# A decoder layer whose input is normalised after the products: roots applied at PSUM, embedding projection moved to the end, one set of gate logits

## The chip, the cores and the metric

The kernel runs on one core of a Trainium2 chip. The metric is device microseconds of that core for one execution, median of several runs. TensorE (PE) multiplies matrices into PSUM; VectorE (DVE), ScalarE (ACT) and GpSimd (POOL) do the element work; SyncE (SP) issues the DMAs.

## The reference, cut to what matters

One decoder layer on 1088 tokens: 1024 of a prompt and 8 x 8 of running samples, width 1024.

```python
proj = rmsnorm(h, norm_mix) @ w_in
qkv, z, b_logit, a_logit, sq, sk, sv, gates = jnp.split(proj, cuts, axis=-1)
o_a, conv_new, s_new = gdn_branch(qkv, z, b_logit, a_logit, ...)   # short conv, silu, gated delta rule, 8 heads
o_b, k_new, v_new = swa_branch(sq, sk, sv, ...)                    # window of 128, 16 query heads on 4 key heads
gates = jax.nn.sigmoid(gates)
h = h + (gates[..., :D] * o_a + gates[..., D:] * o_b) @ w_out
hid = jax.nn.relu(rmsnorm(h, norm_ffn) @ w_up)
h = h + (hid * hid) @ w_down
h = h + jax.nn.sigmoid(rmsnorm(h, norm_ple) @ w_ple_gate) * (p_l @ w_ple_proj)
```

`rmsnorm(x, w)` is `x * rsqrt(mean(x*x) + EPS) * w`: one inverse root per token. It commutes with the product over features: `rmsnorm(x, w) @ W` is `(x * w) @ W` with each token's row times its root.

## The kernel before

Activations lie with features on the 128 partitions and the 1088 tokens along the free dimension, in three chunks of 384, 384 and 320 tokens (`CH`). Every product is done in a split format: an operand is a high part `xh` and a low part `xl`, a weight likewise `wh` and `wl`, and three products (lines 166 to 168) add up high by high, high by low and low by high. A weight tile of 128 output features is used by 8 x 3 products for each chunk. `order` lists all weight tiles; `next_w` keeps three raw loads and one split ahead, and the split costs one ACT copy (L134) and one subtraction (L135, POOL from the third tile on).

Instructions are put in a fixed order per engine when the kernel is built; an engine then works through its own order and waits at semaphores. So what stands behind a waiting instruction on an engine waits too. `side` holds small steps that are dealt out between the products of a tile.

The stages, in order:

1. Head. The embeddings `pT` are split, and `ple(f)` projects them with `wpp` for eight feature tiles; ACT takes each chunk from PSUM (`ppo`, L328) and a DMA stores it in DRAM (`ppd`). Beside that `x_norm(i)` does the input norm of a chunk: ACT squares (L306), DVE sums (L309), `rsqrt_pe` (PE column sums L247, POOL power L251, a ladder of diagonals `dg` L256 and products L257 that spread the roots over the partitions), then x is scaled by root and weight (L316) and split into `xs` (L317, L318).
2. Gate logits: 48 narrow products (L388), transposes (L427, L430), and `gates_tm` twice, once for the prompt and once for the samples, each a chain of small DVE operations; then decay sums by PE (L435 to L454) and a pass through DRAM (`gcd`).
3. Keys. Eight `conv_steps` tiles: ACT takes the chunk from PSUM (`raw`, L500, L502), conv and silu follow. `key_rows` and `key_products` prepare the matrices `kk`, `E` and `LT` of the delta rule. Two feature tiles (`evac_to`, L350) follow.
4. Solve and queries (some 242 to 392 us). Two more tiles by `evac_to` (`qf`, L350) and eight query tiles (`swa_q`, L799 to L805) run on PE, while DVE solves triangular systems in `LT` (`substitute`, L666, L667).
5. Attention (some 392 to 612 us). Eight gate tiles (`gate_tile`, ACT takes the tanh straight from PSUM, L1075), with the attention's steps as side work: scores (L930, L931), DVE scaling and maximum (L934 to L938), exponent on ACT (L940), transposes (L953), values (L975). `swa_keys` and `swa_queries` prepare split keys (`klo`, L888) and queries.
6. Eight delta-rule heads (`gdn_head`): four projection tiles each, the scan as side work.
7. Output projection, norm, MLP in eight blocks, norm, and the gate of the embeddings: for each feature tile `pr` is read back from `ppd`, `ut` is PSUM times root (L1450), tanh, `(ut + 1) * pr` (L1452), added to `h` and stored.

PSUM has eight banks: three `pg` (`ps`) for projections, two `psc`, two `pst`, one `psn`.

## Time and profile before

| | |
|---|---|
| median of 3 runs | 2144.08 us (2135.99 to 2146.12) |
| profiled execution | 2146.7 us |
| its span, first to last instruction | 2144.9 us |
| mean granted PE clock | 0.983 |
| busy: PE, weight loads, DVE, ACT, POOL | 2079.6, 1995.2, 1071.9, 795.5, 718.0 us |
| DMA | 196.5 MB, 92 GB/s mean |

In rows of groups stand line, engine, operation, output and inputs with their shapes, count, then busy time and mean nanoseconds of one, and the idle time before them with what ended it. In rows of waits: who waited, for whom, total us, times, longest. In rows of the timeline: start, duration, engine, line. Products are pipelined, so a product's duration is longer than its share of the engine: the distance between starts is its price.

### The profile page before, as it was taken

How to read it: one execution, taken by the hardware profiler on the slowest of the kernel's cores; microseconds unless marked ns; L12 is line 12 of the kernel's file. 1: busy time of each engine (PE TensorE's matmuls, PEld its weight loads, DVE VectorE, ACT ScalarE, POOL GpSimd, SP SyncE). 2: the span in 40 equal slices, each digit the busy share in tenths (PEclk: the TensorE clock that was granted, in tenths of full speed). 3: DMA queues.
4: the chain of work that ended last, by engine and by line, in shares of the span. 5: the costliest groups of instructions: out<-in, count | busy, mean ns of one | idle time of the engine just before them, and what ended most of it. 6: DMA issues, size and time to landing. Idle time of an engine off the chain costs nothing.

```text
span 2144.9 us, 33830 instructions
## 1 busy us (share of the span) xinstructions
PE 2079.6 (97%) x13597; PEld 1995.2 (93%) x13597; DVE 1071.9 (50%) x1717; ACT 795.5 (37%) x1951; POOL 718.0 (33%) x676
## 2 busy tenths in 40 slices
PE   6999999789999999999999999999999999999999
PEld 6899899668889999999998999999999999999999
DVE  6444499787654555445555444233332323333654
ACT  6476433477643443344334322212131212212411
POOL 3332456243235545454455222212121212121211
PEclk9999999899999999999999999999999999999999
DMA  6365443343243223322242221111111111111132
GB/s 238 122 216 183 116 147 109 104 125 114 85 142 97 76 93 123 108 92 77 93 151 75 77 69 50 40 50 40 50 40 50 40 50 41 49 43 47 40 127 80
DMA packets 89065, 196.50 MB, mean 92 GB/s; under 512 B 33613, under 2 KB 44749, under 8 KB 88781
## 3 DMA queue, kind: packets, MB, share of 16 engines
q1 hardware_dynamic: 88908, 194.35, 27.7%
q8 instruction: 107, 1.75, 0.3%
q14 instruction: 50, 0.40, 0.1%
HBM read 145.48 MB, written 50.78 MB: 91 GB/s over the span
## 4 chain that ended last, share of the span: by engine, by line
PE 80%; DVE 11%; ACT 4%; issue 3%; POOL 2%; DMA 1%; SPq 0%; ACTq 0%; DVEq 0%; POOLq 0%
PE ps L166 23%; PE ps L168 22%; PE ps L167 22%; DVE fs L666 3%; DVE LT L667 3%; PE psn L975 1%; PE pst L953 1%; DVE nm L938 1%; PE psc L1285 1%; ACT pst L572 1%; PE psc L1216 1%; PE psn L1297 1%; PE psc L1290 1%; PE psc L1280 1%; ACT pr L940 1%
## 5 line engine op out<-in xcount | busy, mean ns | idle before, releaser
L135 POOL TENSOR_TENSOR wl<-wr,wh 128x1024 fp32r<-128x1024 f32 x140 | 343.4, 2453 | 909.1 <-ACT wh L134 893.8
L166 PE MATMUL ps<-xh,wh 128*128 128x384 f32 (+1 forms) x1800 | 621.9, 345 | 3.0 <-ACT qf L350 1.6
L167 PE MATMUL ps<-xl,wh 128*128 128x384 f32 (+1 forms) x1800 | 600.1, 333 | 0.0
L168 PE MATMUL ps<-xh,wl 128*128 128x384 f32 (+1 forms) x1800 | 596.7, 332 | 0.0
L166 PEld LDWEIGHTS ps<-xh,wh 128*128 128x128 f32 x1800 | 343.1, 191 | 15.9 <-issue 11.1
L167 PEld LDWEIGHTS ps<-xl,wh 128*128 128x128 f32 x1800 | 343.9, 191 | 1.2 <-issue 1.1
L168 PEld LDWEIGHTS ps<-xh,wl 128*128 128x128 f32 x1800 | 342.1, 190 | 1.6 <-issue 0.7
L134 ACT ACTIVATE wh<-wr 128x1024 fp32r<-128x1024 f32 x143 | 150.8, 1054 | 518.2 <-PE ps L167 441.3
L166 PE MATMUL ps<-uh,wh 128*128 128x384 f32 (+1 forms) x768 | 251.2, 327 | 1.2 <-DVE h L1436 1.2
L168 PE MATMUL ps<-uh,wl 128*128 128x384 f32 (+1 forms) x768 | 251.3, 327 | 0.0
L167 PE MATMUL ps<-ul,wh 128*128 128x384 f32 (+1 forms) x768 | 251.0, 327 | 0.0
L1436 DVE TENSOR_TENSOR h<-h,ps 128x384 f32<-128x384 f32 (+1 forms) x192 | 100.6, 531 | 226.3 <-PE ps L168 226.3
L166 PE MATMUL ps<-ph,wh 128*128 128x384 f32 (+1 forms) x600 | 197.9, 330 | 0.0
L167 PE MATMUL ps<-pl,wh 128*128 128x384 f32 (+1 forms) x600 | 197.6, 329 | 0.0
L168 PE MATMUL ps<-ph,wl 128*128 128x384 f32 (+1 forms) x600 | 197.5, 330 | 0.0
L1422 DVE TENSOR_TENSOR ul<-us,uh 128x384 fp32r<-128x384 f32 (+1 forms) x96 | 98.0, 1022 | 115.2 <-ACT uh L1421 115.2
L166 PEld LDWEIGHTS ps<-uh,wh 128*128 128x128 f32 x768 | 144.3, 188 | 2.0 <-DVE h L1436 2.0
L168 PEld LDWEIGHTS ps<-uh,wl 128*128 128x128 f32 x768 | 144.3, 188 | 0.0
L167 PEld LDWEIGHTS ps<-ul,wh 128*128 128x128 f32 x768 | 144.2, 188 | 0.0
L511 DVE SCALAR_TENSOR_TENSOR cacc<-raw,cw,cacc 128x1112 f32<-128x1112 f32 x72 | 111.1, 1543 | 62.0 <-ACT cacc L509 60.7
L1420 ACT ACTIVATE us<-ut 128x384 f32<-128x384 f32 (+1 forms) x96 | 48.2, 502 | 196.0 <-DVE ut L1419 194.5
L1419 DVE SCALAR_TENSOR_TENSOR ut<-ps,rb 128x384 f32<-128x384 f32 (+1 forms) x96 | 51.3, 535 | 136.5 <-PE ps L168 136.5
(413 smaller groups left out, 3410.4 us busy)
## 6 DMA issues: line engine op xcount, KB each, us to landing
wr<-win SPq DMA_DIRECT2D x60, 512.0 KB
wr<-wup SPq DMA_DIRECT2D x32, 512.0 KB
wr<-wdn SPq DMA_DIRECT2D x32, 512.0 KB
ppd<-ppo SPq DMA_DIRECT2D x8, 544.0 KB
kTd<-kT SPq DMA_DIRECT2D x8, 544.0 KB
Ed<-E SPq DMA_DIRECT2D x8, 544.0 KB
rg<-Ed SPq DMA_DIRECT2D x8, 544.0 KB
gkT<-kTd SPq DMA_DIRECT2D x8, 544.0 KB
```

Source lines behind the costliest of these rows:

```text
L134: act(hv, rv, AF.Copy)
L135: (nc.gpsimd if i > 1 else nc.vector).tensor_tensor(lv, rv, hv.bitcast(F32), ALU.subtract)
L166: mm(ps[:M, :w], a, h[:, c0 : c0 + w], start=(k == 0), stop=False)
L167: mm(ps[:M, :w], a, l[:, c0 : c0 + w], start=False, stop=False)
L168: mm(ps[:M, :w], b, h[:, c0 : c0 + w], start=False, stop=(k == n - 1))
L511: stt(out=cc, in0=raw[:, j : j + CONVW], scalar=cw[:, f, j : j + 1], in1=cc, op0=ALU.mult, op1=ALU.add)
L666: tt(tmp, X[:, j : j + 1, j + 1 :].broadcast_to(sh), X[:, 0:j, j : j + 1].broadcast_to(sh), ALU.mult)
L667: tt(X[:, 0:j, j + 1 :], X[:, 0:j, j + 1 :], tmp, ALU.add)
L1419: stt(out=t, in0=ps[:, :w], scalar=0.0, in1=rb2[:, c0 : c0 + w], op0=ALU.max, op1=ALU.mult)
L1420: act(s, t, AF.Square)
L1422: tt(lo[:, c0 : c0 + w], s, hi[:, c0 : c0 + w].bitcast(F32), ALU.subtract)
L1436: tt(hc, hc, ps[:, :w], ALU.add)
```

## The change

The input's norm is split in two. `x_parts` multiplies x by the norm's weight alone and splits it; `x_roots` computes the roots, spreads them into `rsb` (and per token into `rst`, with its square `rst2`); and every reader of a projection multiplies by `rsb` when it takes the result from PSUM (`scaled`, on DVE). Queries of the prompt stay unscaled: `inverse_lengths` takes the roots into their own norm. The embeddings' split and their products go to the last MLP block and the last stage, where the projection stays in PSUM and is read there. The two sets of gate logits become one of 72 columns. The first conv tile (8) is projected chunk by chunk between the norm's parts, and the rest of the loop over keys is rearranged by one step. In DRAM and SBUF: `cachec` is loaded straight into `cstate`; `kb` shares `kk`; `E` has two buffers; `qraw` is loaded in two halves.

```diff
-    order = [(d["wpp"][u], 1024) for u in range(2)] + [(d["wba"], 128)]
-    order += [(d["win"][f], 1024) for f in WIN_ORDER]
+    order = [(d["win"][f], 1024) for f in WIN_ORDER]
+    order.insert(0, (d["wba"], 128))
...
+        if b == NUP // 4 - 1:
+            ple_order = len(order)
+            order += [(d["wpp"][u], 1024) for u in range(2)]
...
+                if 0 <= i - ple_order < 2:
+                    hi, lo = (xp.tile([P, T], F32R, name=z, tag=t)[:, :1024] for z, t in (("wph", "xh"), ("wpl", "xl")))
...
-            (nc.gpsimd if i > 1 else nc.vector).tensor_tensor(lv, rv, hv.bitcast(F32), ALU.subtract)
+            (nc.gpsimd if i > 2 else nc.vector).tensor_tensor(lv, rv, hv.bitcast(F32), ALU.subtract)
...
+    def scaled(dst, ps, c0, w):
+        tt(dst, ps, rsb[:, c0 : c0 + w], ALU.mult)
     def evac_to(dst):
         def f(c0, w, ps):
-            act(dst[:, c0 : c0 + w], ps[:, :w], AF.Copy)
+            scaled(dst[:, c0 : c0 + w], ps[:, :w], c0, w)
...
         def evac(c0, w, ps):                                  # conv_raw, from conv_steps
             n = min(w, NP - c0)
-            act(raw[:, 3 + c0 : 3 + c0 + n], ps[:, :n], AF.Copy)
+            scaled(raw[:, 3 + c0 : 3 + c0 + n], ps[:, :n], c0, n)
             if n < w:
-                act(rs[:, :, 3:11], ps[:, n:w].rearrange("p (b t) -> p b t", t=8), AF.Copy)
+                v = lambda z: z.rearrange("p (b t) -> p b t", t=8)
+                tt(rs[:, :, 3:11], v(ps[:, n:w]), v(rsb[:, NP:T]), ALU.mult)
...
+        dma(par, d["par"])
+        x_load(0, 0)
+        w_load()
+        x_load(0, 4)
+        w_load()
+        load_constants()
+        for n, (i, k) in enumerate(halves[2:]):
+            x_load(i, k)
+            if n == 1:
+                w_load()
+        dma(cstate, d["cachec"])
+        def x_parts(i):
+            c0, w = CH[i]
+            x = x_in[i]
+            for k in range(KT):
+                hi, lo = (z[:, c0 : c0 + w] for z in xs[k])
+                nk = n_mix[:, k : k + 1]
+                act(hi, x[:, k], AF.Copy, scale=nk)
+                stt(out=lo, in0=x[:, k], scalar=nk, in1=hi.bitcast(F32), op0=ALU.mult, op1=ALU.subtract)
+        def x_roots(i):
+            ...
+            rsqrt_pe(sq[:, 0], c0, w, 1.0 / 1024, EPS, rsb, pp, rst[:, c0 // P :])
+        def logits(i):
+            ...
+            act(ba[:, c0 : c0 + w], ps[:32, :w], AF.Copy)
+        wb, _ = next_w()
+        st8 = tile_steps(xs, conv_raw(8, raw0))
+        for i in range(3):
+            x_parts(i)
+            logits(i)
+            x_roots(i)
+            next(st8)
+        nc.gpsimd.tensor_tensor(rst2, rst[:, 0:8], rst[:, 0:8], ALU.mult)
...
     for h in range(H + 2):
-        st = conv_steps(8 + h, kp, key_tile) if h < H else feature_steps()
-        next(st)
-        if h > 1:
-            key_products(*todo.pop(0))
-        next(st)
-        next(st)
+        if h:
+            st = conv_steps(8 + h, kp, key_tile) if h < H else feature_steps()
+            next(st)
+            next(st)
+            if h > 1:
+                key_products(*todo.pop(0))
+            next(st)
...
                 for e in range(2):                            # swa_q, samples' part
-                    act(qs[:, :, j // 2, (2 * j) % 4 + e], ps[...], AF.Copy)
+                    tt(qs[:, :, j // 2, (2 * j) % 4 + e], v(ps[:, n:w]), v(rsb[:, NP:T]), ALU.mult)
...
-        gemm_tile(xs, lambda c0, w, ps: act(tg[:, c0 : c0 + w], ps[:, :w], AF.Tanh, scale=0.5))
+        def evac(c0, w, ps):                                  # gate_tile
+            t = tg[:, c0 : c0 + w]
+            scaled(t, ps[:, :w], c0, w)
+            act(t, t, AF.Tanh, scale=0.5)
+        gemm_tile(xs, evac)
...
-            act(th, ps[:, :w], AF.Tanh, scale=0.5)            # evac_z
-            stt(out=gt[:, c0 : c0 + w], in0=th, scalar=1.0, in1=ps[:, :w], op0=ALU.add, op1=ALU.mult)
+            scaled(z, ps[:, :w], c0, w)
+            act(th, z, AF.Tanh, scale=0.5)
+            stt(out=z, in0=th, scalar=1.0, in1=z, op0=ALU.add, op1=ALU.mult)
...
-            act(th, ps[:, :w], AF.Tanh, scale=0.5)            # evac_ga
+            scaled(th, ps[:, :w], c0, w)
+            act(th, th, AF.Tanh, scale=0.5)
...
+            wpl, prhs = [next_w() for _ in range(2)], []      # last MLP block
         for u in range(4):
             wh, wl = next_w()
+            if last and u == 2:
+                for k in range(2):
+                    pr = B()
+                    dma(pr, d["pT"][k])
+                    hi = xp.tile([P, T], F32R, name="pph", tag="xh")
+                    lo = xp.tile([P, T], F32R, name="ppl", tag="xl")
+                    act(hi, pr, AF.Copy)
+                    tt(lo, pr, hi.bitcast(F32), ALU.subtract)
+                    prhs.append((hi, lo))
...
+    def ple(f):
+        res = []
+        for i, (c0, w) in enumerate(CH):
+            ps = pst() if i == 2 else psc()
+            ...                                               # six products
+            res.append(ps)
+        return res
+    first = ple(0)
     col_rsqrt_pe(acc, 1.0 / 1024, EPS, rb2, tp)
     for f in range(KT):
-        pr = B()
-        dma(pr, ppd[f])
+        pr = dict(zip((c0 for c0, _ in CH), ple(f) if f else first))
         def evac(c0, w, ps):
             t = tp.tile([P, 384], F32, name="ut", tag="ut")[:, :w]
             tt(t, ps[:, :w], rb2[:, c0 : c0 + w], ALU.mult)
             act(t, t, AF.Tanh, scale=0.5)
-            stt(out=t, in0=t, scalar=1.0, in1=pr[:, c0 : c0 + w], op0=ALU.add, op1=ALU.mult)
+            stt(out=t, in0=t, scalar=1.0, in1=pr[c0][:, :w], op0=ALU.add, op1=ALU.mult)
             hc = hT[f][:, c0 : c0 + w]
-            tt(hc, hc, t, ALU.add)
+            stt(out=hc, in0=t, scalar=0.5, in1=hc, op0=ALU.mult, op1=ALU.add)
```

More of the change, by code (lines that the diff above doesn't have):

```diff
@@ L391, in hybrid_layer @@
     act(ea, alog, AF.Exp)
[L393 to L408 removed]
+    pt = pst()
@@ L409, in gates_tm @@
+    def gates_tm():
+        lg = tmp("lg", 6 * 72).rearrange("p (z n) -> p z n", n=72)
+        b, a, e, s, s2, q = (lg[:, i] for i in range(6))
+        v3 = lambda z: z.rearrange("p (h c) -> p h c", c=9)
+        bc = lambda z, n: z[:, :, None].broadcast_to([P, H, n])
+        part = lambda o: lgt[:, :, o : o + 8].rearrange("p c h -> p h c")
+        tt(v3(a), part(8), part(24), ALU.add)
+        tt(v3(b), part(0), part(16), ALU.add)
+        tt(v3(a), v3(a), bc(dtb, 9), ALU.add)
         stt(out=e, in0=a, scalar=-1.0, in1=a, op0=ALU.mult, op1=ALU.min)
```

270 lines of the change are left out of this document (118 added, 152 removed).

## The prediction

> **What bounds the kernel now.** I read the page first, then busy time and clock by stretches, the waits of PE, and the timeline where these point.
>
> ```profile
> span 2144.9 us, 33830 instructions
> PE 2079.6 (97%) x13597; PEld 1995.2 (93%) x13597; DVE 1071.9 (50%) x1717; ACT 795.5 (37%) x1951; POOL 718.0 (33%) x676
> 0.00:81.10 81.10, 62.77 (x325) 54.62 (x326) 47.28 (x115) 41.12 (x87) 31.08 (x38) 0.89 0.55 191
> 228.00:242.00 14.00, 10.83 (x49) 9.61 (x48) 0.00 (x0) 7.47 (x17) 5.43 (x5) 0.76 0.68 177
> 242.00:376.00 134.00, 134.00 (x849) 132.68 (x849) 123.00 (x135) 49.15 (x111) 75.76 (x37) 0.99 0.35 115
> 376.00:392.00 16.00, 6.96 (x33) 6.16 (x32) 15.66 (x21) 1.38 (x2) 4.04 (x2) 0.65 0.25 82
> 392.00:612.00 220.00, 205.33 (x1733) 174.16 (x1732) 160.91 (x369) 150.22 (x443) 68.23 (x36) 0.99 0.34 107
> 612.00:700.00 88.00, 84.82 (x575) 78.68 (x574) 35.89 (x62) 30.86 (x89) 43.21 (x68) 0.96 0.41 127
> 700.00:1100.00 400.00, 399.89 (x2840) 376.25 (x2839) 199.56 (x331) 158.22 (x470) 206.82 (x296) 1.00 0.30 98
> 2034.00:2056.70 22.70, 21.66 (x110) 20.28 (x109) 7.77 (x18) 4.67 (x7) 5.33 (x5) 0.77 0.19 73
> ```
>
> Each stretch gives its length, then busy time of PE, PEld, DVE, ACT, POOL, the granted clock, DMA share and GB/s. PE bounds the kernel, and no product is added or dropped. So the time can only change where PE is idle or slowed: the head (18.3 us idle, clock 0.89), 228 to 242, 376 to 392 (9 idle, 0.65), the attention (392 to 612, 14.7 idle), 612 to 700 and the last norm. From 242 to 392 DVE is over 90% busy. These waits of PE stand in them:
>
> ```profile
> PE ps L166 <- ACT wh L134: 6.7, 1, 6.7
> PE pst L257 <- DVE dg L256: 4.0, 2, 3.4
> PE ps L166 <- ACT ppo L328: 3.3, 1, 3.3
> PE ps L166 <- ACT qf L350: 1.6, 1, 1.6
> PE pst L435 <- DVE lg L420: 1.7, 1, 1.7
> PE psc L931 <- DVE klo L888: 7.1, 1, 7.1
> PE pst L953 <- ACT pr L940: 6.6, 14, 1.9
> PE ps L166 <- ACT raw L500: 1.4, 1, 1.4
> 61.48 0.44 PE L166 MATMUL ps<-xh,wh 128*128 128x384 f32 x1
> 76.05 0.52 PE L166 MATMUL ps<-xh,wh 128*128 128x384 f32 x1
> 76.37 0.52 PE L167 MATMUL ps<-xl,wh 128*128 128x384 f32 x1
> 80.23 0.31 PE L166 MATMUL ps<-xh,wh 128*128 128x320 f32 x1
> 81.11 0.34 PE L166 MATMUL ps<-xh,wh 128*128 128x384 f32 x1
> 83.74 0.34 PE L166 MATMUL ps<-xh,wh 128*128 128x384 f32 x1
> ```
>
> Starts, not durations, give a product's price: 81.11 to 83.74 is 15 products, 0.175 us each; 80.23 to 81.11 is six of 320 columns, 0.147; and 76.05 to 76.37 is one at the slowed clock, 0.32. So a full projection tile (24 products on each of three chunks) is 48 x 0.175 + 24 x 0.147 = 11.9 us. The first one started at 61.48 and ended at 81.1: 19.6 us, 7.7 too many, because the gate logits' chain sits in it.
>
> **The head.** The embedding projection is 8 tiles of 12 products at 384 columns and 6 at 320: 8 x (12 x 0.175 + 6 x 0.147) = 23.9 us of PE. It leaves the head and comes back at the end at the same price, so it cancels; what counts is when the first w_in tile is done. Before, that is 81.1 - 23.9 = 57.2 without it. The new head is not PE's: logits 32 x 0.175 + 16 x 0.147 = 8 us and one tile, 11.9, are 20 us of products fed by DVE. Its prices:
>
> ```profile
> 0.00:5.00 5.00, 0.00 (x0) 0.00 (x0) 0.11 (x1) 2.02 (x2) 0.19 (x4) 1.00 0.62 200
> L317 ACT ACTIVATE xh<-xc 128x384 fp32r<-128x384 f32 x16 | 7.8, 516 | 6.4 <-DVE xc L316 6.4
> L309 DVE TENSOR_TENSOR xsq<-xsq 128x1536 f32<-128x1536 f32 x2 | 3.5, 1754 | 1.6 <-ACT xsq L306 1.6
> L309 DVE TENSOR_TENSOR xsq<-xsq 128x768 f32<-128x768 f32 x2 | 1.9, 956 | 0.0
> L309 DVE TENSOR_TENSOR xsq<-xsq 128x384 f32<-128x384 f32 x2 | 1.1, 556 | 0.0
> L256 DVE TENSOR_SCALAR dg<-cst,rcomp 128x128 f32<-128x128 f32 x8 | 4.3, 560 | 2.9 <-POOL rcomp L251 2.8
> L134 ACT ACTIVATE wh<-wr 128x1024 fp32r<-128x1024 f32 x4 | 4.2, 1053 | 1.0 <-DMA wr<-wpp 1.0
> L135 DVE TENSOR_TENSOR wl<-wr,wh 128x1024 fp32r<-128x1024 f32 x2 | 2.5, 1225 | 1.2 <-ACT wh L134 1.2
> ```
>
> At 200 GB/s the 0.8 MB of the first half chunk have landed by 4.5 to 5 us (x now stands first on SP's queue; before, two loads of the embeddings and two of its weights stood ahead). The first high part (L317, 0.52) follows, so DVE starts at 5.3. Up to the last low part DVE does: 24 low parts, all on DVE now, at 0.55 (nearest shape, the 128x384 sum; 320 columns 0.47) = 12.6; two of the three sums of squares, 2 x (1.75 + 0.96 + 0.56) = 6.5; low parts of three weight tiles, 2 x 1.23 + 0.3 = 2.8; six diagonals, 3.4; two evictions, 1.1; together 26.4. So the last low part comes at 31.7, the tile's last chunk (24 x 0.147 = 3.5) ends at 35.2, and I add 2 for waits between the engines: 37 (35 to 46). In the sum stands PE's wait for PSUM banks: the tile's evictions need the roots, so the chain sum, PE, POOL, diagonal, PE, copy must end within two chunks; DVE's own queue is longer.
>
> The logits' chain now lies beside the next tile, as one set in place of two. PE's small products stay, DVE's chain about halves: I charge 5 of the 7.7 (2 to 9). Head: 37 + 5 - 57.2 = **-15** (-21 to -3).
>
> **Evictions that go from ACT to DVE.** Nearest rows:
>
> ```profile
> L1436 DVE TENSOR_TENSOR h<-h,ps 128x384 f32<-128x384 f32 (+1 forms) x192 | 100.6, 531 | 226.3 <-PE ps L168 226.3
> L1422 DVE TENSOR_TENSOR ul<-us,uh 128x384 fp32r<-128x384 f32 (+1 forms) x96 | 98.0, 1022 | 115.2 <-ACT uh L1421 115.2
> L500 ACT ACTIVATE raw<-ps 128x384 f32<-128x384 f32 (+1 forms) x72 | 31.9, 446 | 63.4 <-PE ps L168 63.3
> L805 ACT ACTIVATE qs<-ps 64x64 f32<-64x64 f32 x16 | 3.4, 214 | 0.1
> 327.91 3.26 DVE L667 TENSOR_TENSOR LT<-LT,fs 128x992 f32<-128x992 f32 x1
> 332.43 1.19 DVE L667 TENSOR_TENSOR LT<-LT,fs 128x990 f32<-128x990 f32 x1
> ```
>
> A scaled eviction is a DVE product of PSUM and SBUF, 0.53 (L1436); the same length with both inputs in SBUF takes 1.02 (L1422), and a step of the solve 3.26 once and 1.19 next. I take 0.53. The Trainium skill, "SBUF — State Buffer", Who interferes with whom, says that a DVE instruction with two SBUF inputs contends with a GpSimd one that reads SBUF, and one with at most one SBUF input does not; the two rows agree. By it 0.53 holds everywhere; were it 1.02, the attention term below would be about 6 instead of 3.
>
> - Keys (81 to 228): DVE gets 3 x 0.53 + 0.2 per 16 us, and is half idle. ACT gives up as much. The second E buffer and the dropped kb tile only loosen waits; key_products moves one chunk later, hidden by the tile it sits in: -1 (-3 to +2).
> - 228 to 242: PE stood 1.6 for qf, behind ACT's weight split, then ran at half clock. That eviction leaves ACT's queue: of 3.2 idle and 14 x 0.24 = 3.4 of clock I take 4 back: -4 (-6 to 0).
> - Solve (242 to 392): DVE is full, and gets six evictions (3.2) and 16 small ones (at L805's 0.21, 3.4). Behind a waiting DVE queue stand the next solve step and, three banks later, PE. The wait for klo (7.1) is DVE being late at a fixed place in its order, which the change does not remove. I take half of 6.6: +3 (-3 to +8).
> - Attention: 24 x 0.53 = 12.7 on a DVE busy 161 of 220, in front of the softmax steps that PE waits on 14 times (6.6). 14 of 64 steps have no slack now, so about a quarter comes through: +3 (0 to +8). Halved query loads and splits move nothing there.
> - 612 to 700: the raw wait (1.4) and part of the slow clock go: -2 (-4 to 0). From 700 to 1100 PE is busy 399.9 of 400 and DVE half: the 12 evictions per head (6.4) are hidden by products; without that cover they would cost 6.4 a head.
>
> **The end.** The 23.9 are counted. The stores and reloads of the projected embeddings (8 and 8 DMAs, 8.9 MB) go from SP's queue; two loads come in, at a stage with little on the DMAs, but behind weight loads that hold SP until a buffer frees. The first projection stands ahead of the norm and gives PE 3 us more to do while the last feature's squares are summed; against that, two weight tiles and two embedding tiles take operand buffers, so the last three features' splits wait for the last down products, ahead of 9 us of other products. From 2034 to 2056.7, 22.7 us hold one tile of 11.9; the ladder of diagonals stays. Zero (-3 to +6).
>
> **Sum.** -15 - 1 - 4 + 3 + 3 - 2 + 0 = -16. The profiled execution took 2146.7 (span 2144.9), so 2130.7; it was 2.6 above the median of the runs, so 2128 from there. I take 2129.
>
> **Rivals.**
> *The head at half clock.* DVE leaves PE idle over a third of each 10 us chunk. At 0.32 a product, logits and tile need 40 products x 0.32 = 12.8 per chunk, more than DVE: the tile ends at about 5.3 + 12.8 x 2 + 10.7 + 3 = 45, 8 later: 2137. For it: half speed at 76 us, after a stretch of small products with one idle gap of 1.7 (L435); against it: 0.89 over the old head, which was as broken. The Trainium skill, "TensorE: Matmul & The Clock Gate", Part 1, has the clock halved after an idle window of about 3.4 us and restored after a busy one; by that rule gaps of 3 us between chunks mostly keep it, and the trace agrees in that full speed is back at 80 us, 4 us after the slow rows.
> *DVE passes its queue on to PE (the other side).* PE has three banks; from the point where an eviction stands over two chunks, 8.4 us, late in DVE's order, PE waits. Steps that take 3.26 instead of 1.19 make DVE about 2 late each, ten times in 242 to 376: 20, so PE waits 20 - 8.4 = 12, with the 6.6 of added work 19; all 12.7 in the attention come through too: 2129 + 16 + 10 = 2155. Against it: only the last chunk of a query tile and two plain tiles are evicted by DVE there, and PE then waits less for klo.
> *More comes back.* The head keeps to DVE's sum (-2), 228 to 242 and 612 to 700 give all (-4), solve and attention cost nothing (-6): 2117.
> *Nothing in the head:* the 57 stay, if SP's order or the waits for the roots hold x up. I see no row for it; it is the far end of the half-clock case, 2144.
>
> **Chances.** Forecast 0.50 (own range 2119 to 2140), half clock 0.17, DVE 0.15, more 0.18. A measurement of this kernel tells about 0.5%, 10.7 us, from no change: faster is under 2133.4, slower over 2154.8. Faster: 0.18 + 0.40 of the forecast + 0.03; same: 0.10 + 0.14 + 0.03; slower 0.12 of the DVE case. The range goes from below the fourth case to near the DVE case: 2110 to 2150.
>
> **What would show it.** Right: the first w_in tile ends by 34 to 40 us; PE's waits for ppo and qf are gone; the eviction rows read 0.53 on DVE; the stretch with the last norm is about 25 us with a projection in it. Wrong: a head with granted clock near 0.5, PE waiting for evictions between 250 and 390, or more than 14 waits for softmax steps.

## The result, and the profile after

The changed kernel takes 2153.3 us (median of 7 runs, 2151.8 to 2158.7), the kernel before 2140.9 beside it (2136.0 to 2146.1): a ratio of 1.0060, 95% interval 1.0042 to 1.0078. It is slower by 12.4 us. The forecast was a gain, to 2129, with 2150 as the upper end of its range.

The page of the changed kernel: span and busy times.

```profile
span 2151.2 us, 33864 instructions
PE 2076.4 (97%) x13597; PEld 1991.1 (93%) x13597; DVE 1158.7 (54%) x1889; ACT 756.6 (35%) x1819; POOL 707.6 (33%) x690
```

PE does the same products. DVE is busy 87 us longer, ACT 39 us less: the evictions have moved. Their rows, in the groups of DVE:

```profile
L296 DVE TENSOR_TENSOR raw<-ps,rsb 128x384 f32<-128x384 f32 (+1 forms) x72 | 36.7, 510 | 70.1 <-PE ps L178 62.7 <-issue 5.8 <-POOL cstate L327 1.4
L296 DVE TENSOR_TENSOR tg<-ps,rsb 128x384 f32<-128x384 f32 (+1 forms) x30 | 15.9, 530 | 15.1 <-PE ps L178 15.0
L825 DVE TENSOR_TENSOR qs<-ps,rsb 64x64 f32<-64x64 f32 x16 | 3.5, 221 | 0.5
```

The price of one, 0.53 forecast, is right. What they cost is not. The stretches of the changed kernel (length, busy time of PE, PEld, DVE, ACT, POOL, granted clock, DMA share, GB/s), and two of the kernel before that answer to them:

```profile
0.00:37.30 37.30, 25.98 (x144) 20.73 (x145) 25.24 (x48) 25.38 (x40) 3.24 (x9) 1.00 0.65 223
37.30:76.70 39.40, 36.21 (x217) 34.00 (x216) 26.18 (x66) 15.88 (x51) 12.12 (x25) 0.91 0.35 110
332.00:590.80 258.80, 230.78 (x1820) 196.38 (x1820) 197.12 (x422) 159.68 (x463) 88.42 (x63) 0.94 0.34 103
700.00:1100.00 400.00, 394.85 (x2757) 371.38 (x2756) 245.81 (x407) 137.61 (x404) 194.00 (x292) 1.00 0.30 97
```

```profile
81.10:108.90 27.80, 27.68 (x182) 27.35 (x180) 13.72 (x14) 16.99 (x47) 9.12 (x14) 1.00 0.46 156
361.40:606.80 245.40, 221.69 (x1809) 190.68 (x1809) 187.46 (x390) 154.75 (x447) 83.11 (x45) 0.96 0.34 108
```

The first w_in tile ends at 37.3, with DVE busy 25.2 (forecast: 37 and 26.4). The way there is not the forecast's. One row of ACT, then the first and the last low part of that stretch on DVE:

```profile
6.15 1.28 ACT L379 ACT_TABLE_LOAD   x1 [6.15 <-DMA xc<-xT]
8.10 0.62 DVE L380 SCALAR_TENSOR_TENSOR xl<-xc,par,xh 128x384 fp32r<-128x384 f32 x1 [5.25 <-ACT xh L379]
...
35.55 0.54 DVE L380 SCALAR_TENSOR_TENSOR xl<-xc,par,xh 128x320 fp32r<-128x320 f32 x1
```

The first low part starts at 8.1, not 5.3: ACT's first step waited for x until 6.15 and then loaded a table for 1.28. The last low part ends at 36.1, not 31.7, and the tile ends 1.2 behind it, where the sum had 3.5 and another 2. The clock column reads 1.00 here, yet the first 14 products, which start from 8.97 to 13.13, stand 0.32 apart, the distance that the prediction read at the slowed clock; from 13.85 on most stand 0.15 to 0.18 apart.

The next two tiles take 39.4 us where they took 27.8, at a clock of 0.91 in place of 1.00; the stretch of the gate tiles takes 258.8 in place of 245.4 (248.7 in the second profile named below); and in 400 us of the heads PE is idle for 5, where it was idle for 0.1. The waits of PE (total, times, longest) in 250 to 420, and in 620 to 1200, after:

```profile
PE psc L863 <- ACT qf L858: 5.1, 1, 5.1
PE psc L955 <- DVE klo L913: 2.8, 1, 2.8
PE ps L176 <- DVE qs L825: 2.0, 3, 1.1
```

```profile
PE psc L1313 <- DVE S L1328: 6.6, 8, 0.8
```

and in 420 to 620, the waits for softmax steps:

```profile
PE pst L977 <- ACT pr L964: 8.0, 13, 1.6
```

New are the waits for the queries (L863, L825) and for the scan's state S. The wait for `klo`, 7.1 before and 4.3 in the second profile, is 4.8 in two waits over the span, 2.8 of it here. The waits for softmax steps are not more: 13 with 8.0, where the kernel before had 14 with 6.6 in the same window; over the whole span both have 16, with 11.3 after and 8.7 before. So of the signs that the prediction named against itself, one came, waits for evictions between 250 and 390; neither more than 14 waits for softmax steps nor a granted clock near 0.5 over the head did.

The ledger follows from the starts of the w_in tiles on PE (first product `xh` by `wh` of each, tiles counted from 0), with the 23.9 us of embedding products taken off the head of the kernel before and added to its end. A second profile of the kernel before (experiment *before_again*, span 2138.0) stands beside the first, since the first lies at the top of its runs.

| us | forecast | measured, against first profile | against second |
|---|---|---|---|
| first w_in tile done (81.1 and 76.6 before, 37.3 after) | -20 | -19.9 | -15.4 |
| from there to the start of tile 3 (gate chain) | +5 | +11.6 | +11.6 |
| rest of keys, features, 228 to 242 (to tile 12) | -5 | +0.4 | +0.8 |
| solve and attention (tile 12 to tile 28, the first head's) | +6 | +15.8 | +12.4 |
| 612 to 700 (to tile 32) | -2 | -3.3 | -4.8 |
| six heads (tiles 32 to 56) | 0 | +6.4 | +6.5 |
| from there to the end | 0 | -4.6 | +2.2 |
| sum | -16 | +6.4 | +13.3 |

The 11.6 of the second row can be taken apart by the distances between PE's starts. PE is idle for 3.2 where it was idle for 0.1. The 144 products of the two tiles take 28.3 in place of 24.4: 23 of them stand at the slowed clock's distance. And 37 small products of the gate chain and of the last chunk's roots, which the kernel before has ahead of this stretch, take 4.5.

### The profile page after: what moved, and what is told of

Read it like the earlier page. It is cut to its first block, busy times and chain, and to the rows that moved or that the text cites. A ratio compares the mean times of both kernels' runs of the same rounds, so it can differ in the third digit from the quotient of the medians.

```text
span 2151.2 us, 33864 instructions
## 1 busy us (share of the span) xinstructions
PE 2076.4 (97%) x13597; PEld 1991.1 (93%) x13597; DVE 1158.7 (54%) x1889; ACT 756.6 (35%) x1819; POOL 707.6 (33%) x690
## 4 chain that ended last, share of the span: by engine, by line
PE 79%; DVE 9%; ACT 4%; issue 2%; POOL 2%; DMA 1%; SPq 0%; POOLq 0%; ACTq 0%; DVEq 0%
PE ps L176 22%; PE ps L177 22%; PE ps L178 22%; DVE LT L686 2%; DVE fs L685 2%; PE psn L999 1%; DVE cacc L332 1%; PE pst L977 1%; ACT wh L144 1%; DVE gt L1229 1%; PE psc L1323 1%; PE pst L1182 1%; PE psc L1318 1%; PE psc L1313 1%; POOL qst L926 1%
## 5 line engine op out<-in xcount | busy, mean ns | idle before, releaser
L332 DVE SCALAR_TENSOR_TENSOR cacc<-raw,cw,cacc 128x1112 f32<-128x1112 f32 x72 | 121.8, 1692 | 22.6 <-ACT cacc L330 22.1
```

Of the source, the lines that this page charges most:

```text
L332: stt(out=cc, in0=raw[:, j : j + CONVW], scalar=cw[:, f, j : j + 1], in1=cc, op0=ALU.mult, op1=ALU.add)
```

## Experiments

Times are medians; the kernel before, run in turn with each group, gave 2143.1, 2142.6, 2143.7, 2140.4 and 2142.3. Differences to the changed kernel are to its 2153.3, measured with a kernel before of 2140.9. In the short diffs, `act(.., Copy)` stands for the eviction as it was before the change.

### All evictions back on ACT, and their parts

```diff
-            scaled(raw[..], ps[..], c0, n)            # act_all: in every reader of a projection
+            act(raw[..], ps[..], AF.Copy)
```

> The changed kernel, but every reader of a projection takes it from PSUM on ACT as before the change, without the multiplication by the roots (which is left out; the gate logits and the query lengths keep theirs). Theory (the evictions on DVE are what the change pays for): the solve's length returns from 155.6 to about 144 us, the new waits for S in the heads (6.6) go, and the time falls by some 12 + 8 + 4 = 24 us, to about 2129. Rival (the rearranged loop over keys, the halved query loads and the gate logits' chain beside the first key tile cost it): these stay, and the time stays within 5 us of 2153.

Measured: 2122.7, 30.6 us less than the changed kernel (ratio to the kernel before 0.9905, 0.9886 to 0.9924). The evictions cost more than the whole loss. The starts of the tiles place 28.2 of it, the difference of the two profiles: 1.4 up to the end of the first tile, 3.6 from there to tile 3, 6.1 from there to the first query tile, 13.7 from there to the first head, 6.8 in six heads; 3.1 are lost again between (612 to 700), and 0.3 behind. The parts, each alone:

> The changed kernel with the evictions of the eight delta-rule heads alone back on ACT, unscaled (q, v, z and the branch gate lose the multiplication by the roots). Theory: the heads lose 7.7 us because 12 scaled evictions a head stand in DVE's order ahead of the scan's S; without them 1.0 us a head comes back: about 2145.5, and PE's wait for S is gone. Rival (the heads are longer for the clock or for PE's own records, and the products hide the evictions): within 2 us of 2153.

> The changed kernel with the eight gate tiles of the attention back on ACT: the tanh comes straight from PSUM, unscaled. Theory: 24 evictions of 0.53 (12.7 us) leave DVE ahead of the softmax steps, and the head-of-line wait of DVE for a gate tile (4.0) inside the solve goes: 5 to 8 us faster, 2145 to 2148, more of it before 400 us than after. Rival (the attention is bound by PE, ACT and the halved query loads): within 2 us of 2153.

> The changed kernel with the evictions under the solve back on ACT, unscaled: the second pair of feature tiles (6 of 0.5) and the samples' part of the queries (16 of 0.22). Theory: the solve is one chain on DVE, so what leaves DVE there comes off its end one for one: the solve is 5 us shorter, and the time 4 to 6 us less, 2147 to 2149. Rival (the start of the solve is set by the keys, and its end is hidden by gate tiles): within 2 us of 2153.

> The changed kernel with the evictions of the eight key tiles and of the first pair of feature tiles back on ACT, unscaled. With all evictions on ACT the starts of the w_in tiles were ahead of the changed kernel's by 5.0 us at the fourth tile, 7 us at the eighth and 11 us at the first query tile. Theory: all of that comes from these 30 evictions on DVE, between the conv steps and the gate logits' chain: 9 to 13 us faster than the changed kernel, about 2142, and the sum of the four parts (heads 7.9, gates 3.7, solve 5.3, keys 11) is near the 30.6 of all together. Rival (the keys' stretch is bound by PE and the passes through DRAM; the gain of the whole is more than its parts): 0 to 4 us faster.

Measured: heads 2145.3 (-7.9), gate tiles 2149.6 (-3.7), queries and features under the solve 2148.0 (-5.3), keys 2137.5 (-15.8). The four add up to 32.7, the whole gave 30.6. But the parts are not the stages. With the keys' evictions on ACT the first query tile starts 8.8 earlier (209.7); the rest of that gain comes up in the solve and behind it, where the evictions are those of the changed kernel, and why is not shown. The 3.7 of the gate tiles is little more than the kernel before differs by between groups (3.3), but the solve is 3.4 shorter in that profile too.

How an eviction of 0.22 holds PE for 5 us is seen in the changed kernel's timeline of DVE (start, duration). The last query tile's last products end at 332, and two small evictions of it come here:

```profile
330.38 1.08 DVE L686 TENSOR_TENSOR LT<-LT,fs 128x882 f32<-128x882 f32 x1
...
334.74 3.11 DVE L686 TENSOR_TENSOR LT<-LT,fs 128x836 f32<-128x836 f32 x1
337.88 1.00 DVE L685 TENSOR_TENSOR fs<-LT 128x810 f32<-128x810 f32 x1
338.92 1.00 DVE L686 TENSOR_TENSOR LT<-LT,fs 128x810 f32<-128x810 f32 x1
339.95 0.22 DVE L825 TENSOR_TENSOR qs<-ps,rsb 64x64 f32<-64x64 f32 x1
340.09 0.95 DVE L685 TENSOR_TENSOR fs<-LT 128x782 f32<-128x782 f32 x1
341.07 0.23 DVE L825 TENSOR_TENSOR qs<-ps,rsb 64x64 f32<-64x64 f32 x1
```

and ACT's next step, which reads them:

```profile
341.34 1.06 ACT L858 ACTIVATE qf<-qs 64x1024 f32<-64x1024 f32 x1 [7.00 <-DVE qs L825]
```

The eviction stands behind solve steps in DVE's order, one of which took 3.11 where its neighbours took 1.0 (POOL subtracts a weight's high part beside it, from 333.68 to 336.95); ACT waits 7.0 for it, then PE 5.1 (the row L863 above). With this eviction on ACT (*query_act*) the wait for L858 is gone; PE then waits 5.2 for `khi`, made by ACT, but the solve is 5.3 shorter. In the other direction, DVE waited 4.0 for PE once at a gate tile's eviction, with the solve behind it. The solve's steps of the form L686 (count, min/median/max in ns, first and last start), in the kernel before, the changed one, with queries on ACT, and with all on ACT:

```profile
L667 DVE TENSOR_TENSOR LT<-LT,fs x62: 206/974/3257, 259.8 to 403.6; 128x62 f32<-128x62 f32 x2, 128x122 f32<-128x122 f32 x2, 128x180 f32<-128x180 f32 x2, 128x236 f32<-128x236 f32 x2
```

```profile
L686 DVE TENSOR_TENSOR LT<-LT,fs x62: 205/953/3254, 229.4 to 385.2; 128x62 f32<-128x62 f32 x2, 128x122 f32<-128x122 f32 x2, 128x180 f32<-128x180 f32 x2, 128x236 f32<-128x236 f32 x2
```

```profile
L686 DVE TENSOR_TENSOR LT<-LT,fs x62: 207/974/3184, 226.3 to 376.8; 128x62 f32<-128x62 f32 x2, 128x122 f32<-128x122 f32 x2, 128x180 f32<-128x180 f32 x2, 128x236 f32<-128x236 f32 x2
```

```profile
L685 DVE TENSOR_TENSOR LT<-LT,fs x62: 206/958/3233, 216.6 to 359.4; 128x62 f32<-128x62 f32 x2, 128x122 f32<-128x122 f32 x2, 128x180 f32<-128x180 f32 x2, 128x236 f32<-128x236 f32 x2
```

The solve lasts 143.8, 155.8, 150.5 and 142.8: the steps themselves are busy 127.2 before and 128.8 after (both lines of them), so there is more between them. With the gate tiles on ACT it lasts 152.4. Over all kernels of this document, seven profiles without scaled evictions in this stage, the kernel before twice among them, have 142.1 to 145.3; five with all of them on DVE 155.4 to 156.1; three with the scaling on POOL 151.7 to 152.5. But *keys_act*, *keys_act_gates* and *keys_old*, with all of them on DVE, have 150.5 to 154.0: what runs ahead of the solve counts too.

The row "solve and attention" of the ledger is all in the solve. From the first query tile to the solve's last step it is 166.7 after, 153.3 and 153.1 in the two profiles before; from there to the first head 205.6 after, 203.2 and 206.7 before.

### The heads: one operand

> The changed kernel with one operand moved: in the heads' z tiles the scaled value is written back to its PSUM bank, and tanh and the step (th + 1) * z read it there; counts and order of DVE's instructions stay. The output is the full computation. In the kernel before that step read tanh and PSUM and took 0.486 to 0.556; after the change it reads two SBUF operands and took 0.56 to 2.19 (median 1.08), and the scan's S, which PE waits for (0.8 once a head), stands two places behind one of 2.18. Theory (not the added evictions but this second SBUF operand costs the heads): the step is back at 0.5, the 1.1 us a head and the wait for S go: 7 to 8 us faster, 2145 to 2146, as when all the heads' evictions were on ACT. Rival (the 6.4 us a head of evictions crowd DVE): within 2 us of 2153.

```diff
-            z = gt[:, c0 : c0 + w]
-            scaled(z, ps[:, :w], c0, w)
+            z = ps[:, :w]
+            scaled(z, z, c0, w)
             act(th, z, AF.Tanh, scale=0.5)
-            stt(out=z, in0=th, scalar=1.0, in1=z, op0=ALU.add, op1=ALU.mult)
+            stt(out=gt[:, c0 : c0 + w], in0=th, scalar=1.0, in1=z, op0=ALU.add, op1=ALU.mult)
```

Measured: 2142.2, 11.1 less than the changed kernel; ratio to the kernel before 1.0004 (0.9991 to 1.0017). The step's row in the kernel before, in the changed kernel, and with the operand in PSUM (min/median/max in ns):

```profile
L1197 DVE SCALAR_TENSOR_TENSOR gt<-th,ps x24: 486/554/556, 654.4 to 1141.5; 128x384 f32<-128x384 f32 x16, 128x320 f32<-128x320 f32 x8
```

```profile
L1229 DVE SCALAR_TENSOR_TENSOR gt<-th,gt x24: 557/1069/2187, 634.9 to 1128.4; 128x384 f32<-128x384 f32 x16, 128x320 f32<-128x320 f32 x8
```

```profile
L1229 DVE SCALAR_TENSOR_TENSOR gt<-th,ps x24: 486/553/558, 631.8 to 1117.3; 128x384 f32<-128x384 f32 x16, 128x320 f32<-128x320 f32 x8
```

In the changed kernel, in one head (POOL's row first):

```profile
783.10 2.37 POOL L145 TENSOR_TENSOR wl<-wr,wh 128x1024 fp32r<-128x1024 f32 x1 [2.10 <-ACT wh L144]
783.64 2.18 DVE L1229 SCALAR_TENSOR_TENSOR gt<-th,gt 128x320 f32<-128x320 f32 x1 [0.65 <-ACT th L1228]
785.75 0.27 DVE L1290 TENSOR_TENSOR ot<-pst,ot 64x128 f32<-64x128 f32 x1
785.95 0.33 DVE L1328 SCALAR_TENSOR_TENSOR S<-S,egl,psc 128x128 f32<-128x128 f32 x1
```

and the same place with the operand in PSUM:

```profile
778.15 2.38 POOL L145 TENSOR_TENSOR wl<-wr,wh 128x1024 fp32r<-128x1024 f32 x1 [2.09 <-ACT wh L144]
778.65 0.49 DVE L1229 SCALAR_TENSOR_TENSOR gt<-th,ps 128x320 f32<-128x320 f32 x1 [0.61 <-ACT th L1228]
```

S, for which PE waits 0.8, stands two places behind the 2.18. From tile 32 to 56, six heads, the changed kernel takes 413.6, this one 406.4, the kernel before 407.2; PE's wait for S is gone while all 12 evictions a head stay on DVE. So the evictions are hidden there, as forecast; the loss came from the step behind them, whose second input had been PSUM and became SBUF. (Of the 12.0 between the two profiles 7.2 are these heads; 3.8 lie ahead of them, where the order on DVE is the same; what made these is not shown.) This is the rule that the prediction cited from the Trainium skill, "SBUF — State Buffer", Who interferes with whom: a DVE instruction with two SBUF inputs contends with a GpSimd one that reads SBUF, one with at most one such input does not. The trace agrees: of the 24 steps with two SBUF inputs, the 10 with no POOL instruction beside them took 0.56, the 6 beside POOL's `xb` 0.86 to 1.44, and the 8 beside a weight split 2.12 to 2.19; with one input in PSUM all took 0.49 to 0.56, whatever POOL did.

### The gate chain and the keys

> The changed kernel with one order on DVE changed: the first key tile's conv (6 instructions, some 5.6 us) stands behind the gate logits' chain, not between its steps. Theory: the chain from lgt to gs took 15.5 us where its own instructions are about 5; it now takes 8 to 10, PE's wait for gs (1.9) goes and the keys' products follow sooner: the head gives 3 to 6 us back, 2147 to 2150. Rival (the conv is the longer chain: the first key's transposes and products wait for it, so delaying it costs as much): no change or up to 5 us slower.

```diff
+            with tc.issue_after(gate_end.ins):        # gate_end: the instruction that makes gs
                 kT = conv_rest(8, raw0, kp, key_tile)
```

Measured: 2145.2 (-8.1), more than expected. The chain on DVE in the changed kernel, its own steps `lg` between those of the conv and the keys' evictions:

```profile
44.01 0.42 DVE L449 TENSOR_TENSOR lgt<-pst,rst 128x256 f32<-128x256 f32 x1 [1.02 <-PE pst L445]
...
47.85 1.37 DVE L332 SCALAR_TENSOR_TENSOR cacc<-raw,cw,cacc 128x1112 f32<-128x1112 f32 x1
...
49.46 0.59 DVE L466 RECIPROCAL lg<-lg 128x72 f32<-128x72 f32 x1
...
54.06 1.23 DVE L343 SCALAR_TENSOR_TENSOR kT<-raw,cacc 128x1024 f32<-128x1024 f32 x1
...
59.65 0.15 DVE L477 SCALAR_TENSOR_TENSOR gs<-lg,ea 64x8 f32<-64x8 f32 x1
```

and with the conv behind it:

```profile
44.01 0.43 DVE L449 TENSOR_TENSOR lgt<-pst,rst 128x256 f32<-128x256 f32 x1 [1.13 <-PE pst L445]
...
52.91 0.15 DVE L477 SCALAR_TENSOR_TENSOR gs<-lg,ea 64x8 f32<-64x8 f32 x1
```

15.6 us against 8.9. The first query tile starts 7.6 us earlier. But of these only 2.3 lie between the first tile and tile 3 (37.1 in place of 39.4, and 27.8 before); 5.2 lie behind, in the rest of the keys. With the keys' evictions on ACT as well:

> The changed kernel with both the conv behind the gate chain and the evictions of the key and first feature tiles on ACT, unscaled. Alone they gave 8 and 16 us. Theory (both free the same stretch of DVE, 44 to 110 us, where conv steps, evictions and the gate chain stand in each other's way): they do not add up, 2133 to 2139, and the first query tile starts at 207 to 210. Rival (two separate losses): about 2129.

Measured: 2142.2, more than with the evictions alone. They do not add up. The first query tile starts at 207.0, as the theory has it, and up to the third gate tile this kernel is 5.6 ahead of the one with the evictions alone (373.5 against 379.1); at the fourth it is 8.1 behind (423.2 against 415.1). Up to the first query tile 11.5 are gained, by the two edits alone 8.8 and 7.6. What is missing is the gain that the evictions alone had behind it: from the first query tile to the solve's last step 164.9 in place of 161.9 (166.7 in the changed kernel), from there to the first head 205.6 in place of 199.9 (205.6). Why these differ was not settled. The rearranged loop over keys, undone:

```diff
             next(st)
-            next(st)
             if h > 1:
                 key_products(*todo.pop(0))
             next(st)
+            next(st)
...
-        E = kp.tile([P, T], F32, name="E", tag="E")
+        E = kp.tile([P, T], F32, name="E", tag="E", bufs=1)
```

> The changed kernel with key_products back behind the first chunk of the tile and E with one buffer, as before the change. Theory of the evictions: within 2 us of 2153. Rival (the loop over keys, moved by a chunk, costs the time between 37 and 200 us): 4 us faster or more.

Measured: 2158.1 (+4.9; ratio to the kernel before 1.0077, 1.0060 to 1.0094, where the changed kernel has 1.0042 to 1.0078). So the rearrangement is no part of the loss; that it helps is likely, but the intervals overlap.

### The other parts of the change

```diff
-                act(hi, x[:, k], AF.Copy, scale=nk)
-                stt(out=lo, in0=x[:, k], scalar=nk, in1=hi.bitcast(F32), op0=ALU.mult, op1=ALU.subtract)
+                stt(out=x[:, k], in0=x[:, k], scalar=n_mix[:, k : k + 1], in1=rs[:, :w], op0=ALU.mult, op1=ALU.mult)
+                act(hi, x[:, k], AF.Copy)
+                (nc.vector if k % 4 == 0 else nc.gpsimd).tensor_tensor(lo, x[:, k], hi.bitcast(F32), ALU.subtract)
...
-            x_parts(i)
+            x_parts(i, x_roots(i))                    # roots first; evictions as in act_all
             logits(i)
-            x_roots(i)
```

> Everything of the change except its first part: x is normalised before the products (as before the change: roots first, x times root and weight, split, three quarters of the low parts on POOL), so no projection is scaled and all evictions are on ACT; the embeddings at the end, the one set of gate logits, the first key tile chunk by chunk and the loop over keys stay as changed. The output is the full computation. Theory: the stages from 80 us on run as with all evictions on ACT (2122.7); the first key tile ends some 5 to 10 us later, since roots and 24 scalings of 0.55 stand ahead of the products: 2127 to 2134, faster than the kernel before (2143) and than the changed one. Rival (the early products are what the change gains, so the head is as long as before, 57 us, and the evictions were only hidden behind it): 2143 or more.

Measured: 2150.6 (ratio 1.0033, 1.0021 to 1.0044): the rival. The first w_in tile ends at 60.0, where it ended at 57.2 before without the embeddings' share. Its stretches from 40 to 60:

```profile
40.00:50.00 10.00, 9.28 (x36) 6.18 (x36) 7.31 (x13) 4.56 (x9) 6.66 (x7) 0.66 0.01 2
50.00:60.00 10.00, 8.83 (x58) 7.14 (x56) 5.08 (x10) 4.69 (x12) 6.12 (x12) 1.00 0.00 0
```

From this and *act_all* the first part of the change is worth 2150.6 - 2122.7 = 27.9 us (24.1 at the end of the first tile, 60.0 against 35.9, and 24.1 between the spans of the two profiles), and its evictions cost 30.6. The rest of the change costs 8 against the kernel before. One part of that rest alone, on the kernel before:

```diff
-        for step in (0, 1, 2, n0, n1, n0, n0, 3, n1, n2, n1, 4, 5, n2, n2, 6, 7):
+        for step in (n0, n1, n0, n0, n1, n2, n1, n2, n2):    # ple, its weights and pT: as in the changed kernel
```

> The kernel before with one part of the change alone: the embedding projection at the end. The norm stays ahead of the products, with two sets of gate logits and the keys' loop as before. The output is the full computation. The prediction took 23.9 us out of the head with the projection, as if PE were the head's bound. Theory (the norm's chain of DVE, ACT and POOL is the bound, and the projection was hidden in its gaps): the head keeps most of its 61.5 us, the first tile ends at 70 to 78 (not 57), and the time is 10 to 20 us longer less the 5.5 gained in the last norm: 2147 to 2158. Rival (the head is as long as its products, the 8 us of the normalised variant are the gate logits and the keys): first tile ends at 57 to 60, 2135 to 2141.

Measured: 2154.2 (ratio 1.0068, 1.0049 to 1.0087). The first tile ends at 69.3: 11.8 earlier than in the first profile of the kernel before and 7.3 earlier than in the second, not 23.9. (The profiled execution, 2161.0, is the slowest of its runs.) PE's first wait there:

```profile
PE psn L255 <- DMA cst<-cst: 14.5, 1, 14.5
```

So half or more of the embedding products had been filling gaps of the old head, this wait for constants probably among them. Moved alone, they are a loss of 13.8.

The conv behind the gate chain (the edit of *gates_ahead*), in the normalised variant:

> The kernel that normalises x before the products (2150.6) with the one order on DVE changed: the first key tile's conv behind the gate logits' chain. The output is the full computation. In it the starts of the tiles lost 10 us to the kernel before between the first and the third tile, where PE waited 4.4 for g and the conv's steps stand between the chain's. Theory (the one set of gate logits is slowed by the conv that now runs beside it): 5 to 9 us faster, 2142 to 2146. Rival (the loss is that the keys' loop starts with its transposes and products late, whatever the chain does): within 2 us of 2150.6.

Measured: 2153.9, not faster. The chain took 9.1 us in place of 15.5, yet tile 4 starts level (112.8 against 112.6) and the first query tile 4.4 later. So the chain was not what the keys waited for in that kernel; what they wait for stays open.

### Remedies

```diff
-            n = 4
-            while n:
-                tt(sq[:, 0:n], sq[:, 0:n], sq[:, n : 2 * n], ALU.add)
-                n //= 2
...
+                for k in range(KT):                   # in rsqrt_pe, in place of one product for the sum
+                    mm(ps[:m, c : c + 1], acc[:, k, c * P : c * P + m], ones[:, 0:1], start=(k == 0), stop=(k == KT - 1))
```

> The changed kernel with the conv behind the gate chain (2145.2), and the sums of squares of x taken from DVE: PE adds the eight feature blocks up in PSUM (72 products of one column in place of 9). The output is the full computation. Theory (DVE is what the head waits for): 9.7 us of sums leave DVE, 6.5 of them ahead of the first tile's end; PE's products of one column take some 0.1 to 0.2 each while it waits anyway: the first tile ends 3 to 6 us earlier and the time is 2139 to 2143. Rival (PE's own order and the landing of x set the head): within 2 us of 2145.

> x normalised before the products, the conv behind the gate chain, and the sums of squares on PE. The output is the full computation. In the first of these the second chunk's roots stood late because DVE's order had the third chunk's first sum (which waits for ACT) ahead of the second chunk's last one (3.4 us), and the first chunk's sums ran from 9.8 to 14.2. Theory: without these sums the first product starts some 3 us and the first tile ends 8 to 12 us earlier than at 60.0; with the gate chain's part some 15 us off 2150.6: 2133 to 2139, below the kernel before. Rival (ACT, POOL's low parts at 1.3 each and the wide spread of roots set the head): 2142 or more.

Measured: 2160.6 and 2168.4, both far slower. The stretch 50 to 60 of the first, and its one-column products in 46 to 53:

```profile
50.00:60.00 10.00, 10.00 (x48) 9.07 (x49) 4.25 (x13) 2.81 (x4) 5.24 (x15) 0.51 0.01 2
```

```profile
L260 PE MATMUL psn<-cst,xsq x42: 165/250/265, 45.8 to 51.2; 128*128 128x1 f32 x26, 128*64 128x1 f32 x16
```

DVE's time fell by 10.4 against the kernel without this edit, as expected, but the first tile ends at 57.0, not at 31 to 34. The 72 products stand in the trace as 144 instructions, and by the distances between starts these hold PE for 17.5 us, where the expectation's 0.1 to 0.2 for each of 72 is 7 to 14. To that comes the clock: PE reads busy from 10 us on, but the granted clock is 0.71 in 20 to 30 and 0.51 here.

```diff
     def scaled(dst, ps, c0, w):                       # all but the first key tile
-        tt(dst, ps, rsb[:, c0 : c0 + w], ALU.mult)
+        act(dst, ps, AF.Copy)
+        nc.gpsimd.tensor_tensor(dst, dst, rsb[:, c0 : c0 + w], ALU.mult)
```

> The changed kernel with the conv behind the gate chain (2145.2) and all scaled evictions but the first key tile's moved off DVE: ACT copies from PSUM as before the change, and POOL multiplies by the roots in SBUF, about 1 us for 128x384 (POOL took 2.46 for 128x1024); the samples' queries are scaled by POOL at the end of the stage. The output is the full computation. Theory (only the place in DVE's order makes the evictions dear; POOL is a third busy): most of the 17 us of solve, attention and heads and some of the keys' come back: 2128 to 2136. Rival (POOL is slower beside DVE and holds up the weight splits and the norms of the scan that stand behind it in its own order): 2145 or more.

Measured: 2211.6. Between the first query tile and the first head tile it loses 4.4 against the kernel before, where the changed kernel loses 15.8; but each head is 8.2 us longer than in the changed kernel (six heads 462.7 in place of 413.6). POOL has 12 more steps of about 1.0 in each, and PE now waits for the scan's `r`, `q` and `psn`, 28 us in six heads; that these stand behind POOL's scalings is argued, not tested.

> The changed kernel with the conv behind the gate chain (2145.2), and POOL scaling only between 210 and 590 us: the second pair of feature tiles, the samples' queries and the gate tiles are copied from PSUM by ACT and multiplied by POOL; keys and heads keep their evictions on DVE. The output is the full computation. With all evictions on POOL that stretch (start of the first query tile to start of the first head tile) lost 4.4 us against the kernel before, where the scaled evictions on DVE lose 17.0. Theory: 10 to 13 us come back: 2132 to 2136, faster than the kernel before (2143). Rival (what is saved there is lost at 590 us to the softmax steps or the first head): 2141 or more.

```diff
-            scaled(t, ps[:, :w], c0, w)               # gate tiles; likewise features, queries
+            act(t, ps[:, :w], AF.Copy)
+            nc.gpsimd.tensor_tensor(t, t, rsb[:, c0 : c0 + w], ALU.mult)
```

Measured: 2140.0, 5.2 less than without it, half of what was expected: the stretch from the first query tile to the first head gives 9.8 back, but that tile starts 2.8 later. It is level with the kernel before (0.9991, 0.9978 to 1.0003).

> The kernel with the conv behind the gate chain and POOL scaling between 210 and 590 us (2140.0), with the same operand moved to PSUM in the heads. The output is the full computation. Theory: the heads' loss of 1.1 us each goes here too, 7 to 8 us faster: 2132 to 2133, faster than the kernel before (2140 to 2144). Rival (another wait takes its place): 2138 or more.

Measured: 2128.3; ratio to the kernel before 0.9939 (0.9919 to 0.9959). This version, of three remedies on the change, beats both kernels, by 14 and 25 us:

```profile
span 2127.0 us, 33915 instructions
```

The kernel before, once more:

> The kernel before, unchanged, for a second profile: its first one (2146.7) lies at the top of its runs (2131 to 2148). If the spread of the runs is all over the kernel, every stage differs by its share; if it is one place, the starts of the tiles part there.

Measured: 2139.8, span 2138.0. The starts part in the head (first tile done 4.5 us earlier, all of it lost again by tile 32, which starts at 685.1 in both), in the output projection (2.7) and in the last norm (4.0). There, the first profile and the second:

```profile
2040.00:2060.00 20.00, 19.87 (x98) 18.81 (x99) 6.92 (x20) 3.67 (x7) 4.76 (x5) 0.74 0.19 74
```

```profile
2040.00:2060.00 20.00, 19.85 (x123) 19.14 (x123) 11.04 (x23) 4.73 (x9) 4.61 (x4) 1.00 0.27 88
```

The same program does 98 products in this stretch at a clock of 0.74, or 123 at 1.00.

## Why the prediction was wrong

Two terms of the sum failed, and both were steps of DVE priced by their own length. The evictions were put at 6 us, 3 in the solve, 3 in the attention and nothing in keys and heads, on the ground that DVE has idle time or that products cover them; back on ACT they are worth 30.6 (in the heads by one operand, not by the evictions themselves). The gate chain was put at 5, and its stretch lost 11.6. Step by step:

- *First tile at 37.* The end is right, 37.3, and so nearly is DVE's work, 25.2 for 26.4; but part of it is luck. DVE started 2.8 late and its last low part came 4.4 late, while of the 5.5 behind it 1.2 were needed. The half-clock rival fell but for the first 14 products, about 2 us (14 x 0.145).
- *"DVE's chain about halves: I charge 5 of the 7.7."* Failed: 11.6. I counted the chain's own instructions, not what stands between them in DVE's order: the conv of the first key tile now comes ready at the same time, and the chain takes 15.6, without it 8.9. Yet with the conv behind the chain this stretch gets only 2.3 back, of 8.1 in the whole kernel. The larger parts are the three read from PE's starts: products moved into the stretch 4.5, slowed products 3.9, idle 3.1. Why the clock falls there no run separates.
- *Keys: "DVE gets 3 x 0.53 + 0.2 per 16 us, and is half idle ... -1".* Failed: from tile 3 to the first query tile -5 was forecast with 228 to 242, and 0.4 to 0.8 were lost. With all evictions on ACT that row is 135.7, in place of 141.8 after and 141.4 before: the gain was there, and 6.1 of evictions took it. A half idle DVE did not mean that an eviction is done when PE ends.
- *Solve +3, attention +3.* For the solve the mechanism was right and the size off: 13.4 to 13.6. For the attention the term was not borne out: the stretch behind the solve is as long as before, within what two profiles differ by, and the softmax waits are no more. What the gate tiles' evictions cost lies in the solve, under which the first of them fall. The point that the rival named (an eviction 8.4 us late) was about reached at the last query tile, whose products end at 332.0 and whose last eviction ends at 341.3. This rival, DVE passing its queue on to PE, is the one that happened in the solve, though PE waited less for its three banks (2.0, L825) than for the step that ACT makes of the queries (5.1). That its 2155 is 2 us from the result is luck: it had nothing for the keys and the heads, kept the head's full gain, and put 32 on solve and attention, which lost 12.4 to 15.8.
- *Heads: "the 12 evictions per head (6.4) are hidden by products".* They are. But the step behind three of them lost its PSUM operand, and I costed only instructions that were added, not those whose operands moved. 6.4 for six heads.
- *"By it 0.53 holds everywhere."* True of the evictions, and the same rule spoke against this change one line further down in the diff.
- *228 to 242 (-4), 612 to 700 (-2).* PE's waits for `ppo` and for the old `qf` eviction went; but from the last feature tile to the first query tile it is 17.7 us in place of 18.2 (17.7 in the second profile), so these 4 did not come; the second gave 3.3 to 4.8.
- *End: zero.* Against the first profile the last part gains 4.6, against the second it loses 2.2, with the clock of the last norm at 0.74 and 1.00 in these. The zero stands within what two executions of one program differ by.

## What to carry to other kernels

Cost an eviction that is moved to another engine by its place in that engine's order: what stands ahead of it, and who waits for it; here the engine's idle share did not tell. Go through the diff for instructions that stay but read from another memory: in the heads one operand that went from PSUM to SBUF cost 7.2 us, and a dozen added instructions per head cost nothing that showed. And before a change is put down to a stage, take the profile of the old kernel twice: here two executions of it differed by 7 us.

## What the runs showed of the hardware

Runs of products with one moving column go with a lower granted clock, though PE reads busy without a gap: in the changed kernel with such sums, each of three runs of 40 instructions (4.4 to 6.2 us) was overlapped or followed within 1.1 us by a stretch at half clock, with 0.51 in 50 to 60. The clock in a short stretch of dependent small work differs between executions of one program (0.74 and 1.00 in the last norm). And a DVE step of 128x320 with both inputs in SBUF took 2.18 beside a subtraction of POOL on 128x1024, where it takes 0.49 with one input in PSUM beside the same subtraction; with both in SBUF and POOL idle, a step of 128x384 took 0.56.
